# Steps of a chunked scan traced at their places in a stream of dense matmuls, one turn four triples later, and a scaling moved behind a convolution

## The chip, the cores and the metric

The kernel runs on one core of a Trainium2 chip. The metric is the device time of one execution in microseconds (us). The kernel before was timed three times. The profile is of one further execution, and times within it count from the start of its span.

## The reference

One hybrid encoder over 512 tokens of width 1024: a Mamba-2 layer, then a differential attention layer, all in fp32. The change lies in the first layer, cut here to what matters:

```python
def mamba2_layer(x, norm_g, w_in, conv_w, conv_b, dt_bias, a_log, d_skip, gate_norm_g, w_out):
    h = rms_norm(x, norm_g)
    zxbcdt = h @ w_in                                   # z | x | B | C | dt
    ...
    xbc = jax.nn.silu(causal_depthwise_conv(xbc, conv_w, conv_b))
    xs, bm, cm = ...                                    # 8 groups: 4 heads of 64, state 128
    dt = jax.nn.softplus(dt_raw + dt_bias)
    a = -jnp.exp(a_log)
    y = ssd_chunked_scan(xs * dt[..., None], a * dt, bm, cm)
    y = y + d_skip * xs
    y = gated_group_rms_norm(y, z, gate_norm_g)         # y * silu(z), norm within a group
    return x + y @ w_out
```

The scan, per chunk: `y = (C B^T * decay) x + (C state) * exp(acs)` and `state = state * exp(acs_end) + B^T (x * to_end)`, where `acs` is the running sum of `a * dt`. The second layer (shared K/V, queries, two softmax maps per head, ALiBi, a gate and an output projection) and the final norm follow.

## The kernel before

**Dense stream.** A product in fp32 precision is made of three matmuls on operands split into a high and a low part (`mm3`: high times high, high times low, low times high). I call three such matmuls a triple. The first layer's projections are one stream of triples, in the order `z0 g0 g1 z1 g2 g3 z2 g4 o0 g5 z3 g6 g7 o1 o2 o3`: `z` is a quarter of z, token-major (32 triples), `g` one group's B, C and two halves of x, feature-major (32 triples), `o` a quarter of the output projection. Each item fills four PSUM banks of a pool of four (`mm`), named pz, pg and po in the trace. A bank is free again when its last reader is done: for pz ScalarE's silu (zs), for po VectorE's add to x_tok, for pg VectorE's convolution.

**Weights.** Each item has two loads of 1 MB (raw). ScalarE writes the high part, scaled by the norm's gain (whi, four pieces), and VectorE the low part (wlo). Raw, whi and wlo have two buffers each, so whi of an item waits until TensorE has used the weights two loads earlier.

**Convolution.** `conv` takes a bank pg: VectorE scales it by the norm's row, ScalarE starts xc with one tap and the bias, VectorE adds three taps (scalar_tensor_tensor, 511, 510 and 509 columns wide), ScalarE applies silu. The step with 509 columns is the last to read the bank. B's tile is the first of a group, then C's, then the two of x.

**Scan.** `ssd(g)` handles one group in steps, with TensorE's part of each: `cb` (C B^T, into pcb), `bt` (three transposes of B, pbt), `xt` (eight transposes of x, pxt; VectorE then scales x into xdt and dx), `st` (state products psA and psB on xe, which GpSimd makes from xdt; then 64 small products pyd), `o1` and `o2` (state times C, po1 and po2; VectorE scales them into tmp), and `yt`, the turn (pyt): eight transposes of the normed result tmp, read by ScalarE into yh and by VectorE into yl. Between o2 and yt lies the gated norm: GpSimd adds tmp to dx, VectorE multiplies by zs, ScalarE squares, VectorE takes a root in ten small steps (v, y_i, y_y, y_c), ScalarE writes the scaled tmp. `decays` loads the running sums of a group (dec), and GpSimd subtracts and masks them (four affine selects), ScalarE takes exp. Scan banks come from a pool of three (`ss`) and one bank of their own (`long`).

**Order.** A table, PLACES, gives each step of each group a number of triples after the end of that group's projection. In the kernel before, a group's whole scan is written when its projection has been written; the wrapper `Ordered` logs TensorE's instructions with their step, and `in_places` sorts the log by the table and chains TensorE's instructions in that order. On the other engines a scheduler orders instructions by the dependencies and the order in which the code wrote them.

Of the kernel before, what the change touches and what calls it, by code (L numbers as in the profile page):

```python
# [22 lines left out]
G = 8  # L23
# [24 lines left out]
    "y0": (None,) * 7 + (69,),  # L48
# [15 lines left out]
class Ordered:  # L64


    def __init__(self, tc, engine):
        self.tc, self.engine, self.on = tc, engine, False
        self.step, self.log = None, None

    def __getattr__(self, name):
        op = getattr(self.engine, name)

        def call(*args, **kw):
            i = op(*args, **kw)  # L75
            if self.on:
                self.tc.keep_in_program_order(i)
            elif self.log is not None:
                self.log.append((self.step, i.ins))
            return i  # L80
# [5 lines left out]
def trunk(ctx, tc, x, x_t, par, w_dt, w_in, w_out, w_kvqg, w_bo, d_skip, lam_qk, fin_g, out):  # L86
# [405 lines left out]
    ps_tt = ss_bank("ps_tt")  # L492
    for i, src in enumerate((dtp, acs, toe)):
        T.transpose(ps_tt[:, i * P:(i + 1) * P], src, ident)
    tok = const.tile([P, 4, NQ, H], F32, name="tok")
    V.tensor_copy(tok[:, 0:3].rearrange("p a c h -> p (a c h)"), ps_tt[:, 0:3 * P])
    A.activation(tok[:, 3], tok[:, 1], AF.Exp)
    dt_tok, acs_tok, toe_tok, eacs_tok = (tok[:, i] for i in range(4))


# [18 lines left out]

    def conv(ps, ft, name, bufs):  # L520
# [7 lines left out]
        for k in (2, 1, 0):  # L528
            d = 3 - k
            V.scalar_tensor_tensor(out=xc[:, d:], in0=u[:, :S - d], scalar=cw[k], in1=xc[:, d:], op0=ALU.mult, op1=ALU.add)  # L530
# [44 lines left out]
    def stream_a():  # L575
        for it in order_a[1:]:
            j = int(it[1])
            yield from {"z": z_proj, "g": group_proj, "o": out_proj}[it[0]](j)
            done.add(it)
            ends[it] = sum(step is None for step, i in T.log)  # L580
        while True:
            yield

    ends = {}

    def in_places(log):

        dense = [i for step, i in log if step is None]
        parts = {}
        for step, i in log:  # L590
            if step:
                parts.setdefault(step, []).append(i)
        due = sorted((ends[f"g{g}"] + 3 * PLACES[kind][g], n, kind, g) for n, (kind, g) in enumerate(parts))
        order = []
        for n, i in enumerate(dense + [None]):
            while due and due[0][0] <= n:
                order += parts[due.pop(0)[2:]]
            order.append(i)
# [27 lines left out]
    def ssd(g):  # L626
# [5 lines left out]
        T.step = "cb", g  # L632
# [4 lines left out]
        T.step = "bt", g  # L637
# [26 lines left out]
        T.step = "st", g  # L664
# [58 lines left out]
        for j, a in [(j, a) for a in range(0, NQ, n) for j in range(2)]:  # L723
            T.step = f"y{a}" if g == G - 1 else "yt", g
# [512 lines left out]
```

## Time and profile before

| | |
|---|---|
| median of three runs | 713.04 us (712.07 to 714.62) |
| profiled execution | 712.19 us, span 710.4 us |
| TensorE busy | 697.7 us (98%) |
| VectorE busy | 520.5 us (73%) |
| ScalarE busy | 426.9 us (60%) |
| GpSimd busy | 113.9 us (16%) |
| dense matmul, 128x512 | 390 to 403 ns each, pipelined |
| TensorE clock granted | full in all 40 slices |

In a row of the timeline the first number is the start, the second the time from the start of the first to the end of the last instruction of that row, then engine, line, operation, output and inputs, and count. Brackets give the engine's idle time ahead and what ended it. All operations of TensorE, VectorE and ScalarE stand on line 75, the wrapper's call, so tiles identify them. Matmul ends are modelled and overlap, so the distance between starts shows the pace.

### The profile page before, as it was taken

To read this page: it belongs to the slowest core of one execution; us is meant where nothing else is said; L and a number is where in the kernel's file an instruction comes from. 1 tells how busy PE (TensorE), PEld (TensorE's weight loads), DVE (VectorE), ACT (ScalarE), POOL (GpSimd) and SP (SyncE) were. 2 spreads that over 40 slices of the span, in tenths; PEclk is the share of its full clock that TensorE was granted. 3 is DMA by queue.
4 is the path that set the end of the run, shared out by engine and by line. 5 is a ranking of instruction groups with operands and counts; after the bars stand their busy time and mean duration, and the time that the engine had idled before them with its cause. 6 is when DMAs were issued, how large, how long until landed. Compare 5 with 4: busy or idle time off the path is not lost.

```text
span 710.4 us, 10484 instructions
## 1 busy us (share of the span) xinstructions
PE 697.7 (98%) x3838; PEld 579.8 (82%) x3838; DVE 520.5 (73%) x1181; ACT 426.9 (60%) x931; POOL 113.9 (16%) x158
## 2 busy tenths in 40 slices
PE   8999999999999999999999999999999999999996
PEld 7878878887788888888788878888888888888884
DVE  5579964888579669558996856457768657788786
ACT  6839662664653636537635347557777667765556
POOL 0108421502405025041110101000000000000002
PEclk9999999999999999999999999999999999999999
DMA  8643313333043241231122310322211221113003
GB/s 293 254 172 130 119 59 120 118 118 120 16 163 119 83 150 66 97 140 60 60 69 110 119 60 17 149 81 88 91 60 66 82 90 60 62 57 119 31 1 118
DMA packets 13491, 70.85 MB, mean 100 GB/s; under 512 B 1792, under 2 KB 3328, under 8 KB 6016
## 3 DMA queue, kind: packets, MB, share of 16 engines
q1 hardware_dynamic: 13008, 69.90, 26.8%
q8 instruction: 30, 0.49, 0.3%
q10 hardware_dynamic: 432, 0.28, 0.1%
q14 instruction: 21, 0.17, 0.1%
HBM read 68.02 MB, written 2.16 MB: 99 GB/s over the span
## 4 chain that ended last, share of the span: by engine, by line
PE 91%; DVE 4%; ACT 2%; issue 1%; POOL 1%; DMA 1%; ACTq 0%; POOLq 0%
PE pg L75 23%; PE po L75 16%; PE pz L75 10%; PE pt L75 7%; PE pq L75 6%; PE pk L75 6%; PE pv L75 6%; PE pb L75 3%; PE sc L75 3%; PE pyd L75 2%; PE pc L75 2%; PE psA L75 1%; DVE xc L75 1%; PE pcb L75 1%; DVE wlo L75 1%
## 5 line engine op out<-in xcount | busy, mean ns | idle before, releaser
L75 DVE SCALAR_TENSOR_TENSOR wlo<-raw,prm,whi 128x512 fp32r<-128x512 f32 (+1 forms) x240 | 149.5, 672 | 53.5 <-ACT whi L75 52.7
L75 ACT ACTIVATE whi<-raw,prm 128x512 fp32r<-128x512 f32 (+1 forms) x240 | 133.6, 628 | 52.2 <-PE pg L75 11.7
L75 PE MATMUL pg<-a_hi,whi 128*128 128x512 f32 x256 | 103.2, 403 | 0.1
L75 PE MATMUL pg<-a_hi,wlo 128*128 128x512 f32 x256 | 100.2, 391 | 0.1
L75 PE MATMUL pg<-a_lo,whi 128*128 128x512 f32 x256 | 99.9, 390 | 0.0
L75 DVE SCALAR_TENSOR_TENSOR xc<-pg,prc,xc 128x511 f32<-128x511 f32 (+2 forms) x96 | 69.8, 740 | 6.6 <-ACT xc L75 6.1
L75 PEld LDWEIGHTS pg<-a_hi,wlo 128*128 128x128 f32 x256 | 48.1, 188 | 11.0 <-DVE wlo L75 0.5
L75 PEld LDWEIGHTS pg<-a_hi,whi 128*128 128x128 f32 x256 | 48.1, 188 | 10.2 <-issue 0.7
L75 PEld LDWEIGHTS pg<-a_lo,whi 128*128 128x128 f32 x256 | 48.2, 188 | 9.4
L75 PE MATMUL po<-whi,yh 128*128 128x512 f32 x128 | 51.6, 403 | 1.3 <-DVE xc L75 1.3
L75 PE MATMUL pz<-whi,a_hi 128*128 128x512 f32 x128 | 49.8, 398 | 1.7 <-DVE xc L75 1.3
L75 PE MATMUL po<-whi,yl 128*128 128x512 f32 x128 | 50.1, 391 | 0.0
L75 PE MATMUL po<-wlo,yh 128*128 128x512 f32 x128 | 50.0, 390 | 0.0
L75 PE MATMUL pz<-whi,a_lo 128*128 128x512 f32 x128 | 48.9, 390 | 0.0
L75 PE MATMUL pz<-wlo,a_hi 128*128 128x512 f32 x128 | 48.9, 390 | 0.0
L1042 POOL TENSOR_TENSOR ot<-x_tok,fg 128x512 f32<-128x512 f32 x4 | 5.0, 1292 | 248.9 <-DVE x_tok L75 248.9
L75 ACT ACTIVATE s<-s,mx 128x128 f32<-128x128 f32 (+3 forms) x64 | 35.6, 557 | 10.1 <-DVE mx L75 10.0
L657 POOL TENSOR_TENSOR xe<-xdt,tok 128x256 f32<-128x256 f32 x24 | 14.1, 615 | 165.0 <-DVE xdt L75 165.0
L75 DVE CUSTOM_DVE_ANT_0 s<-sc,bias 128x128 f32<-128x128 f32 (+3 forms) x64 | 29.3, 487 | 15.3 <-PE sc L75 14.8
L75 ACT ACTIVATE xc<-pg,prc 128x512 f32<-128x512 f32 x32 | 24.8, 776 | 25.3 <-DVE pg L75 19.9
L75 ACT ACTIVATE xc<-xc 128x512 f32<-128x512 f32 x32 | 20.0, 629 | 27.0 <-DVE xc L75 22.5
L75 ACT ACT_TABLE_LOAD x23 | 29.5, 1283 | 10.6 <-DVE xc L75 9.1
(238 smaller groups left out, 1629.9 us busy)
## 6 DMA issues: line engine op xcount, KB each, us to landing
raw<-in_w_in SPq DMA_DIRECT2D x22, 1024.0 KB, 4.8
raw<-in_w_kvqg SPq DMA_DIRECT2D x16, 1024.0 KB, 4.8
dec<-acs_d SPq DMA_DIRECT2D x8, 1024.0 KB, 4.9
raw<-in_w_out SPq DMA_DIRECT2D x8, 1024.0 KB, 4.8
raw<-in_w_bo SPq DMA_DIRECT2D x4, 1024.0 KB, 4.8
x_tok<-in_x SPq DMA_DIRECT2D x4, 512.0 KB, 8.9
out<-ot SPq DMA_DIRECT2D x6, 256.0 KB, 2.1
raw<-in_w_in SPq DMA_DIRECT2D x4, 256.0 KB, 4.7
```

The source lines that it names most:

```text
L75: i = op(*args, **kw)
L657: GP.tensor_tensor(out=xe[:, c], in0=xdt[:, c], in1=toe_tok[:, c, hs].unsqueeze(2).to_broadcast([P, R, HD]), op=ALU.mult)
L1042: GP.tensor_tensor(out=o, in0=y, in1=f, op=ALU.mult)
```

## The change

The steps of the scan become yields of `ssd`: a step is written when the stream of triples has come to its place (`first_layer`, `resume`), and TensorE simply keeps program order, so that the log and the sorting are gone. The transposition of dt and the sums (`turned`, ps_tt), with the first two `decays`, becomes such a step at triple 22. The table moves group 0's bt from 3 to 10, group 0's turn from 56 to 60 and group 1's bt from 24 to 28 (the same place in the stream as that turn). Group 7's first turn keeps 69, in a row shared with the others. Where steps fall on one triple, the older group's came first; now the order follows from when the steps were entered in the queue and how long it was then. In the built order the younger group's step comes first at groups 2 and 3 (pcb3 before po12 and po22, pbt3 before pyt2) and at groups 6 and 7 (pcb7 before po16, pbt7 before pyt6). And x's scaling (xdt, dx) may be issued only after the last convolution step of the next group's B tile, where that is already written.

```diff
@@ -39,13 +39,12 @@
 PLACES = {
     "cb": (10, 2, 14, 14, 5, 5, 14, 12),
-    "bt": (3, 24, 21, 44, 35, 25, 21, 37),
+    "bt": (10, 28, 21, 44, 35, 25, 21, 37),
     "xt": (16, 35, 31, 52, 43, 36, 31, 43),
     "st": (25, 47, 37, 63, 53, 47, 36, 53),
     "o1": (28, 47, 46, 64, 54, 47, 44, 53),
     "o2": (32, 52, 46, 69, 60, 52, 47, 58),
-    "yt": (56, 85, 76, 99, 89, 85, 69, None),
-    "y0": (None,) * 7 + (69,),
+    "y0": (60, 85, 76, 99, 89, 85, 69, 69),
     "y2": (None,) * 7 + (72,),
 }
@@ -489,14 +485,17 @@
         z_out(0, t, pz0[t])
-    ps_tt = ss_bank("ps_tt")
-    for i, src in enumerate((dtp, acs, toe)):
-        T.transpose(ps_tt[:, i * P:(i + 1) * P], src, ident)
     tok = const.tile([P, 4, NQ, H], F32, name="tok")
-    V.tensor_copy(tok[:, 0:3].rearrange("p a c h -> p (a c h)"), ps_tt[:, 0:3 * P])
-    A.activation(tok[:, 3], tok[:, 1], AF.Exp)
     dt_tok, acs_tok, toe_tok, eacs_tok = (tok[:, i] for i in range(4))
+    def turned():
+        yield "tt"
+        ps_tt = ss_bank("ps_tt")
+        for i, src in enumerate((dtp, acs, toe)):
+            T.transpose(ps_tt[:, i * P:(i + 1) * P], src, ident)
+        V.tensor_copy(tok[:, 0:3].rearrange("p a c h -> p (a c h)"), ps_tt[:, 0:3 * P])
+        A.activation(tok[:, 3], tok[:, 1], AF.Exp)
+        decays((0, 1))
     def runs_of(kind):
@@ conv @@
+    conv_end = {}
...
@@ -527,7 +528,7 @@
         A.activation(xc, u, AF.Identity, scale=cw[3], bias=prc[:, ft:ft + 1])
         for k in (2, 1, 0):
             d = 3 - k
-            V.scalar_tensor_tensor(out=xc[:, d:], in0=u[:, :S - d], scalar=cw[k], in1=xc[:, d:], op0=ALU.mult, op1=ALU.add)
+            conv_end[ft] = V.scalar_tensor_tensor(out=xc[:, d:], in0=u[:, :S - d], scalar=cw[k], in1=xc[:, d:], op0=ALU.mult, op1=ALU.add)
         A.activation(xc, xc, AF.Silu)
         return xc
@@ -572,34 +573,30 @@
                     sq = small.tile([P, S], F32, tag="wide", name=f"sq3_{t}", bufs=2)
                     A.activation(sq, x_tok[:, t, ns], AF.Square, accum_out=bss[:, 0, t:t + 1])
-    def stream_a():
+    due = []
+
+    def resume(n, at, gen, places):
+        kind = next(gen, None)
+        if kind is not None:
+            due.append((at + places[kind], len(due), at, gen, places))
+
+    def first_layer():
+        n = 0
         for it in order_a[1:]:
             j = int(it[1])
-            yield from {"z": z_proj, "g": group_proj, "o": out_proj}[it[0]](j)
-            done.add(it)
-            ends[it] = sum(step is None for step, i in T.log)
-        while True:
-            yield
-
-    ends = {}
-
-    def in_places(log):
-
-        dense = [i for step, i in log if step is None]
-        parts = {}
-        for step, i in log:
-            if step:
-                parts.setdefault(step, []).append(i)
-        due = sorted((ends[f"g{g}"] + 3 * PLACES[kind][g], n, kind, g) for n, (kind, g) in enumerate(parts))
-        order = []
-        for n, i in enumerate(dense + [None]):
-            while due and due[0][0] <= n:
-                order += parts[due.pop(0)[2:]]
-            order.append(i)
-        order.pop()
+            for _ in {"z": z_proj, "g": group_proj, "o": out_proj}[it[0]](j):
+                n += 1
+                due.sort(key=lambda e: e[:2])
+                while due and due[0][0] <= n:
+                    place, _, at, gen, places = due.pop(0)
+                    with tc.high_priority() if places.get("last") else ExitStack():
+                        resume(n, at, gen, places)
+                    due.sort(key=lambda e: e[:2])
+            if it[0] == "g":
+                places = {kind: p[j] for kind, p in PLACES.items()}
+                places["last"] = j == G - 1
+                resume(n, n, ssd(j), places)
         assert not due
-        for i, before in zip(order[1:], order):
-            tc.add_manual_dep(i, before.name, mybir.DependencyInfo(mybir.DependencyClass.NoSync, mybir.DependencyReason.DATA), reason="order")
     bss = small.tile([P, 2, NT], F32, name="bss", bufs=1)
     decs = {}
@@ -642,16 +639,18 @@
         A.copy(bt.rearrange("p c n -> p (c n)"), pbt[:, 0:3 * P])
         xdt = bp.tile([P, NQ, R, HD], F32, tag="xdt", name=f"xdt{g}")
         dx = bp.tile([P, NQ, R, HD], F32, tag="dx", name=f"dx{g}")
-        T.step = "xt", g
+        yield "xt"
         for j in range(2):
             pxt = ss_bank(f"pxt{g}_{j}")
             for c in range(NQ):
                 T.transpose(pxt[:, c * P:(c + 1) * P], xc[j][:, c * P:(c + 1) * P], ident)
             pv = pxt.rearrange("p (c h e) -> p c h e", h=2, e=HD)
             h2 = slice(R * g + 2 * j, R * g + 2 * j + 2)
-            V.tensor_tensor(out=xdt[:, :, 2 * j:2 * j + 2, :], in0=pv, in1=dt_tok[:, :, h2].unsqueeze(3).to_broadcast([P, NQ, 2, HD]), op=ALU.mult)
-            V.tensor_tensor(out=dx[:, :, 2 * j:2 * j + 2, :], in0=pv,
-                            in1=dsk[:, h2].unsqueeze(1).unsqueeze(3).to_broadcast([P, NQ, 2, HD]), op=ALU.mult)
+            next_b = conv_end.get(17 + g)
+            with tc.issue_after(next_b.ins) if next_b else ExitStack():
+                V.tensor_tensor(out=xdt[:, :, 2 * j:2 * j + 2, :], in0=pv, in1=dt_tok[:, :, h2].unsqueeze(3).to_broadcast([P, NQ, 2, HD]), op=ALU.mult)
+                V.tensor_tensor(out=dx[:, :, 2 * j:2 * j + 2, :], in0=pv,
+                                in1=dsk[:, h2].unsqueeze(1).unsqueeze(3).to_broadcast([P, NQ, 2, HD]), op=ALU.mult)
         xe = bp.tile([P, 3, R, HD], F32, tag="xe", name=f"xe{g}")
         for c in range(3):
             GP.tensor_tensor(out=xe[:, c], in0=xdt[:, c], in1=toe_tok[:, c, hs].unsqueeze(2).to_broadcast([P, R, HD]), op=ALU.mult)
@@ -721,29 +720,19 @@
         n = 2 if g == G - 1 else NQ
         for j, a in [(j, a) for a in range(0, NQ, n) for j in range(2)]:
-            T.step = f"y{a}" if g == G - 1 else "yt", g
+            if not j:
+                yield f"y{a}"
             for c in range(a, a + n):
                 T.transpose(pyt[j][:, c * P:(c + 1) * P], tm[:, c, j * P:(j + 1) * P], ident)
             cs = slice(a * P, (a + n) * P)
             A.copy(yh[:, j, cs], pyt[j][:, cs])
             V.tensor_tensor(out=yl[:, j, cs], in0=pyt[j][:, cs], in1=yh[:, j, cs].bitcast(F32), op=ALU.subtract)
         yT[g] = (yh, yl)
-        T.step = None
-
-    decays((0, 1))
-    dense[0] = stream_a()
-    T.log = []
-    for g in range(G):
-        until(f"g{g}")
-        if g < G - 1:
-            ssd(g)
-        else:
-            with tc.high_priority():
-                ssd(g)
-    until("o3")
-    in_places(T.log)
-    T.log = None
-
+
+    T.on = True
+    resume(0, 0, turned(), {"tt": 22})
+    first_layer()
+    T.on = False
     hh, hl = new_h("b")
     done.clear()
```

**ScalarE around group 0's turn**, in z1. zs is the silu of z, whi8 and whi9 are weights of g2. Before:

```order
L75 ACTIVATE tmp0_697<-dx0_662,y_y_754 128x256 x4
L75 CAST yh0_770<-pyt0_0_772 128x512
L75 CAST yh0_770<-pyt0_1_773 128x512
L75 COPY bt1_947<-pbt1_943 128x384
L75 ACTIVATE whi8_924<-raw8_922,prm_70 128x512 x4
L75 ACTIVATE zs1_2_0_1218<-pz1_2_1173,ar_col_239 128x256
```

and with the change:

```order
L73 ACTIVATE tmp0_798<-dx0_702,y_y_883 128x256 x4
L73 ACTIVATE whi8_912<-raw8_910,prm_70 128x512 x4
L73 ACTIVATE zs1_2_0_1055<-pz1_2_990,ar_col_239 128x256
L73 ACTIVATE zs1_2_1_1057<-pz1_2_990,ar_col_239 128x256
L73 CAST yh0_899<-pyt0_0_901 128x512
L73 CAST yh0_899<-pyt0_1_902 128x512
```

The turn's readers yh and the copy of bt now stand behind the four pieces of whi8 and the two halves of zs1_2. On TensorE the turn itself moved from behind the third triple of pz1_3 to behind the last triple of pz1_2, twelve matmuls later.

**VectorE at the end of g3**, ahead of z2. xc19 is B's tile on bank pg3_0, xc27 C's on pg3_1, xc6 one of x's. Before:

```order
L75 SCALAR_TENSOR_TENSOR xc19_1620<-pg3_0_1402,prc_72,xc19_1620 128x510
L75 SCALAR_TENSOR_TENSOR xc27_1633<-pg3_1_1551,prc_72,xc27_1633 128x510
L75 TENSOR_TENSOR xdt2_1417<-pxt2_0_1419,tok_438 128x4x128
L75 TENSOR_TENSOR dx2_1418<-pxt2_0_1419,dsk_344 128x4x128
L75 SCALAR_TENSOR_TENSOR xc19_1620<-pg3_0_1402,prc_72,xc19_1620 128x509
L75 TENSOR_TENSOR xdt2_1417<-pxt2_1_1426,tok_438 128x4x128
L75 TENSOR_TENSOR dx2_1418<-pxt2_1_1426,dsk_344 128x4x128
L75 SCALAR_TENSOR_TENSOR xc6_1652<-pg3_2_1588,prc_72,xc6_1652 128x511
L75 SCALAR_TENSOR_TENSOR xc27_1633<-pg3_1_1551,prc_72,xc27_1633 128x509
```

and with the change:

```order
L73 SCALAR_TENSOR_TENSOR xc19_1497<-pg3_0_1390,prc_72,xc19_1497 128x510
L73 SCALAR_TENSOR_TENSOR xc27_1510<-pg3_1_1403,prc_72,xc27_1510 128x510
L73 SCALAR_TENSOR_TENSOR xc19_1497<-pg3_0_1390,prc_72,xc19_1497 128x509
L73 TENSOR_TENSOR xdt2_1492<-pxt2_0_1545,tok_434 128x4x128
L73 TENSOR_TENSOR dx2_1493<-pxt2_0_1545,dsk_344 128x4x128
L73 TENSOR_TENSOR xdt2_1492<-pxt2_1_1552,tok_434 128x4x128
L73 TENSOR_TENSOR dx2_1493<-pxt2_1_1552,dsk_344 128x4x128
L73 SCALAR_TENSOR_TENSOR xc6_1529<-pg3_2_1440,prc_72,xc6_1529 128x511
L73 SCALAR_TENSOR_TENSOR xc27_1510<-pg3_1_1403,prc_72,xc27_1510 128x509
```

The last step on bank pg3_0 (xc19, 128x509) moved ahead of both xdt and dx; the last step on pg3_1 stays where it was. VectorE's order at the end of g7, ahead of o1, changes in the same way.

**VectorE in z2, before g4.** v42, y_i, y_y and y_c are the root of group 2's norm, and wlo14 and wlo15 are weights of g4. Before:

```order
L75 TENSOR_TENSOR y_c_1511<-y_y_1510,v42_1508 128x4
L75 TENSOR_TENSOR y_c_1511<-y_c_1511,y_y_1510 128x4
L75 SCALAR_TENSOR_TENSOR y_c_1511<-y_c_1511 128x4
L75 SCALAR_TENSOR_TENSOR y_y_1510<-y_c_1511,y_y_1510 128x4
L75 TENSOR_TENSOR y_c_1511<-y_y_1510,v42_1508 128x4
L75 TENSOR_TENSOR y_c_1511<-y_c_1511,y_y_1510 128x4
L75 SCALAR_TENSOR_TENSOR y_y_1510<-y_c_1511,y_y_1510 128x4
L75 SCALAR_TENSOR_TENSOR wlo14_1681<-raw14_1678,prm_70,whi14_1680 128x512 x4
L75 SCALAR_TENSOR_TENSOR wlo15_1895<-raw15_1892,prm_70,whi15_1894 128x512 x4
```

and with the change:

```order
L73 TENSOR_TENSOR y_c_1724<-y_y_1723,v42_1721 128x4
L73 SCALAR_TENSOR_TENSOR wlo14_1582<-raw14_1579,prm_70,whi14_1581 128x512
L73 TENSOR_TENSOR y_c_1724<-y_c_1724,y_y_1723 128x4
L73 SCALAR_TENSOR_TENSOR wlo14_1582<-raw14_1579,prm_70,whi14_1581 128x512
L73 SCALAR_TENSOR_TENSOR y_c_1724<-y_c_1724 128x4
L73 SCALAR_TENSOR_TENSOR wlo14_1582<-raw14_1579,prm_70,whi14_1581 128x512
L73 SCALAR_TENSOR_TENSOR y_y_1723<-y_c_1724,y_y_1723 128x4
L73 SCALAR_TENSOR_TENSOR wlo14_1582<-raw14_1579,prm_70,whi14_1581 128x512
L73 TENSOR_TENSOR y_c_1724<-y_y_1723,v42_1721 128x4
L73 TENSOR_TENSOR y_c_1724<-y_c_1724,y_y_1723 128x4
L73 SCALAR_TENSOR_TENSOR y_y_1723<-y_c_1724,y_y_1723 128x4
L73 SCALAR_TENSOR_TENSOR wlo15_1667<-raw15_1664,prm_70,whi15_1666 128x512 x4
```

The four pieces of wlo14 now stand between the steps of the root, where they stood behind its last step. A little ahead of these rows, dec3 times pcb3 now comes before tmp2, as pcb3 now comes before po12 and po22 on TensorE. ScalarE's squares of the last two quarters (ss42) moved from ahead of the exponential of dec4 to behind it, and GpSimd does three of dec4's four masks ahead of its first addition for group 2.

More of the change, by code (lines that the diff above doesn't have):

```diff
@@ L68, in __init__ @@
         self.tc, self.engine, self.on = tc, engine, False
-        self.step, self.log = None, None
     def __getattr__(self, name):
@@ L77, in call @@
                 self.tc.keep_in_program_order(i)
-            elif self.log is not None:
-                self.log.append((self.step, i.ins))
             return i
@@ L630, in ssd @@
         hs = slice(R * g, R * g + R)
-        T.step = "cb", g
+        yield "cb"
         pcb = long_bank(f"pcb{g}")
@@ L636, in ssd @@
             T.matmul(pcb[:, cs], lhsT=bc[:, cs], rhs=cc[:, cs], start=True, stop=True)
-        T.step = "bt", g
+        yield "bt"
         pbt = ss_bank(f"pbt{g}")
@@ L663, in ssd @@
         psA = ss_bank(f"psA{g}")
-        T.step = "st", g
+        yield "st"
         for c in range(2):
@@ L690, in ssd @@
             decays((g + 1, g + 2))
-        T.step = "o1", g
+        yield "o1"
         po1 = ss_bank(f"po1{g}")
         T.matmul(po1[:, 256:512], lhsT=cc[:, P:2 * P], rhs=hsf[:, 0], start=True, stop=True)
-        T.step = "o2", g
+        yield "o2"
         po2 = ss_bank(f"po2{g}")
@@ L774, in last_rows @@
             row_norm(t, po)
-    due = [0.0]
+    owed = [0.0]
     def beside(n):
-        due[0] += n
-        while due[0] > 0:
-            due[0] -= next(dense[0], due[0])
+        owed[0] += n
+        while owed[0] > 0:
+            owed[0] -= next(dense[0], owed[0])
     T.on = V.on = A.on = True
@@ L971, in trunk @@
     dense[0] = paced(stream_b())
-    due[0] = 0.0
+    owed[0] = 0.0
     beside(8)
@@ L1076, in trunk @@
     until("q0t0")
-    due[0] = 0.0
+    owed[0] = 0.0
     last = None
```

## The prediction

> **What bounds the kernel now.** I read the page's busy times first, then TensorE's own waits, then the timeline around each wait.
>
> ```profile
> span 710.4 us, 10484 instructions
> PE 697.7 (98%) x3838; PEld 579.8 (82%) x3838; DVE 520.5 (73%) x1181; ACT 426.9 (60%) x931; POOL 113.9 (16%) x158
> PE pyt L75 <- ACT tmp L75: 1.5, 1, 1.5
> PE pz L75 <- DVE xc L75: 1.3, 1, 1.3
> PE po L75 <- DVE xc L75: 1.3, 1, 1.3
> ```
>
> TensorE sets the time: it is without work for only 710.4 - 697.7 = 12.7 us. Work taken from another engine is worth nothing unless it ends a wait of TensorE. The three waits shown are the only ones inside the first layer; the others lie at the kernel's start and in its tail, which the diff does not touch. So the change is worth what it does to these three, less any wait it makes.
>
> **Part 1: group 0's last turn, four triples later.** Here is TensorE at the turn (pyt), with an undisturbed turn of group 2 below it.
>
> ```profile
> 99.38 0.39 PE L75 MATMUL pz<-whi,a_lo 128*128 128x512 f32 x1
> 101.27 1.97 PE L75 MATMUL pyt<-ident,tmp 128*128 128x128 f32 x8 [1.51 <-ACT tmp L75]
> 103.32 0.47 PE L75 MATMUL pz<-whi,a_hi 128*128 128x512 f32 x1
> 199.01 1.04 PE L75 MATMUL pyt<-ident,tmp 128*128 128x128 f32 x8
> 200.13 0.48 PE L75 MATMUL pg<-a_hi,whi 128*128 128x512 f32 x1
> ```
>
> The idle figure says 1.51, but the starts say more. Dense matmuls start 0.23 apart (twelve of them from 162.75 to 165.54, rows in part 2), and a free turn with its three transposes of bt takes 200.13 - 199.01 = 1.12. From 99.38 to 103.32 there are 3.94, so this turn lost 3.94 - 0.23 - 1.12 = **2.59 us**: the transposes that follow also wait, one by one, for ScalarE's four writes of tmp, and count as busy meanwhile. The Trainium skill (Perfetto Trace Analysis, Identifying the Most-Contended Engine) warns that matmul busy time misleads because matmuls are pipelined; the trace agrees here, 1.51 idle against 2.59 lost. By the idle figure alone the sum below would be 2.86 instead of 3.94.
>
> Does tmp come early enough for the new place? The turn would start at 99.38 + 0.23 + 12 x 0.23 = 102.37. ScalarE and VectorE around it:
>
> ```profile
> 100.71 1.71 ACT L75 ACTIVATE tmp<-dx,y_y 128x256 f32<-128x256 f32 x4 [0.77 <-DVE y_y L75]
> 102.84 1.08 ACT L75 CAST yh<-pyt 128x512 fp32r<-128x512 f32 x2 [0.42 <-PE pyt L75]
> 104.29 2.56 ACT L75 ACTIVATE whi<-raw,prm 128x512 fp32r<-128x512 f32 x4
> 106.76 0.81 ACT L75 ACTIVATE zs<-pz,ar_col 128x256 f32<-128x256 f32 x2
> 103.46 1.29 DVE L75 TENSOR_TENSOR yl<-pyt,yh 128x512 fp32r<-128x512 f32 x2 [2.78 <-ACT yh L75]
> 110.92 1.04 PE L75 MATMUL pxt<-ident,xc 128*128 128x128 f32 x8
> ```
>
> The first transpose started 0.13 after the first quarter of tmp could be done (100.71 + 0.43 = 101.14). The fourth quarter ends at 102.42, so it is usable at 102.55; the fourth transpose comes at 102.37 + 3 x 0.10 = 102.67. No wait is left, with 0.12 to spare. What is late next is the reading of the turn: ScalarE now does the next weights' four whi and two zs first (102.42 + 2.47 + 0.81 = 105.70), then yh, and VectorE's first yl starts 0.62 after yh (102.84 to 103.46) and takes 0.65: 106.97. Queued behind are TensorE's transposes of x for group 1 (pxt), the next to need that bank, at 110.92 - 2.59 = 108.33. Cover 1.36 us; beyond it each us is a us of TensorE. I take the full 2.59; the lower bound is the plain idle of 1.51. The weights themselves gain, since whi now starts at 102.42 instead of 104.29. Group 0's bt and the three start-up transposes (ps_tt) only move among dense matmuls of 0.23 and nobody waited for them: 0, between -0.1 and +0.15, a switch or so saved.
>
> **Part 2: x's scaling behind the next group's first bank.** The scaling moves at two places only, ahead of z2 and ahead of o1. First place, VectorE and TensorE:
>
> ```profile
> 160.67 0.68 DVE L75 TENSOR_TENSOR xdt<-pxt,tok 128x512 f32<-128x512 f32 x1
> 161.87 0.73 DVE L75 SCALAR_TENSOR_TENSOR xc<-pg,prc,xc 128x509 f32<-128x509 f32 x1
> 162.52 0.68 DVE L75 TENSOR_TENSOR xdt<-pxt,tok 128x512 f32<-128x512 f32 x1
> 163.72 1.39 DVE L75 SCALAR_TENSOR_TENSOR xc<-pg,prc,xc 128x511 f32<-128x511 f32 x2
> 162.75 0.47 PE L75 MATMUL pz<-whi,a_hi 128*128 128x512 f32 x1 [1.30 <-DVE xc L75]
> 165.54 0.39 PE L75 MATMUL pz<-whi,a_hi 128*128 128x512 f32 x1
> ```
>
> TensorE starts 162.75 - 161.87 = 0.88 after the last convolution step of B's bank starts. That step moves into the place of the first xdt, 160.67, so z2 starts at 161.55: 1.20 earlier. But z2 wants its second bank 165.54 - 162.75 = 2.79 later, at 164.34, and that bank is freed by the second of the two steps at 163.72, which starts at 164.38 and does not move, since the work ahead of it is the same: 164.38 + 0.88 = 165.26. A new wait of 0.92 takes the place of most of the old one, and z2 keeps **0.28**. The second xdt still starts at 162.52, so GpSimd's xe, which waits for it, is not late.
>
> Second place:
>
> ```profile
> 346.74 0.68 DVE L75 TENSOR_TENSOR xdt<-pxt,tok 128x512 f32<-128x512 f32 x1
> 347.93 0.73 DVE L75 SCALAR_TENSOR_TENSOR xc<-pg,prc,xc 128x509 f32<-128x509 f32 x1
> 349.78 1.39 DVE L75 SCALAR_TENSOR_TENSOR xc<-pg,prc,xc 128x511 f32<-128x511 f32 x2
> 348.81 0.47 PE L75 MATMUL po<-whi,yh 128*128 128x512 f32 x1 [1.30 <-DVE xc L75]
> 351.66 1.03 PE L75 MATMUL psA<-xe,bt 128*128 128x256 f32 x4
> 355.07 0.50 PE L75 MATMUL po<-whi,yh 128*128 128x512 f32 x1
> 349.35 1.76 POOL L657 TENSOR_TENSOR xe<-xdt,tok 128x256 f32<-128x256 f32 x3 [26.60 <-DVE xdt L75]
> ```
>
> Again 0.88 behind the step (347.93 to 348.81), now from 346.74: o1 starts at 347.62, **1.19** earlier. Here the second bank is wanted only after the scan's psA, psB and pyd, at 355.07 - 1.19 = 353.88, and is free at 349.78 + 0.66 + 0.88 = 351.32. The third is released by the add of o1's first bank to x_tok, which stood at 355.00 and now stands one row earlier; o1 wants it four triples of 0.68 after 353.88, at 356.60. Next to be late is xe: its second part ends at 349.35 + 2 x 0.59 = 350.53, and psA's second product now falls at 351.66 - 1.19 + 0.22 = 350.69. That is 0.16 of cover. I take 1.19; bounds 0.28, if a bank is waited for as at z2, and 1.30, the idle shown.
>
> **Part 3: exchanged ties.** Where two steps fall on one triple, the younger group's now goes first: pcb before po, pbt before pyt (groups 2/3 and 6/7). At groups 2/3 this reorders VectorE, GpSimd and ScalarE ahead of g4's weights:
>
> ```profile
> 181.35 0.64 POOL L619 TENSOR_SCALAR_AFFINE_SELECT dec<-dec 128x512 f32<-128x512 f32 x1
> 181.96 0.74 POOL L707 TENSOR_TENSOR dx<-dx,tmp 128x256 f32<-128x256 f32 x1
> 184.80 1.61 POOL L619 TENSOR_SCALAR_AFFINE_SELECT dec<-dec 128x512 f32<-128x512 f32 x2
> 182.73 0.83 DVE L75 TENSOR_TENSOR dx<-dx,zs 128x256 f32<-128x256 f32 x1 [1.95 <-POOL dx L707]
> 186.47 1.28 ACT L75 ACT_TABLE_LOAD   x1
> 189.59 2.54 ACT L75 ACTIVATE whi<-raw,prm 128x512 fp32r<-128x512 f32 x4
> 190.33 2.74 DVE L75 SCALAR_TENSOR_TENSOR wlo<-raw,prm,whi 128x512 fp32r<-128x512 f32 x4 [1.89 <-ACT whi L75]
> 191.14 0.50 PE L75 MATMUL pg<-a_hi,wlo 128*128 128x512 f32 x1
> ```
>
> GpSimd now does three masks (0.61 each, 181.35 to 181.96), one dx (0.68) and the last mask (0.64): 184.50 instead of 184.80 + 1.61 = 186.41. ScalarE's square of the product that follows dx (183.86 + 0.05, then 0.83, then 0.42) ends at 185.2; table load and exp take 189.59 - 186.47 = 3.12, two squares that stood ahead of them now follow, 0.42 each: whi starts at 189.2, 0.4 sooner. VectorE's wlo now stands between the small steps of the root: four of 0.2 ahead, first wlo at 190.0 (was 190.33), then one per 0.66 + 0.12, the fourth at 192.36 (was 190.33 + 3 x 0.66 = 192.31). TensorE's use follows wlo by 0.81 (190.33 to 191.14): fourth at 193.17, where before its pace gave 191.14 + 3 x 0.73 = 193.33. So of the 0.28 won at z2 **0.16** stays. The norm of tmp now ends behind whi (2.45), a load (1.30), zs, whi and zs (4.1) and itself (1.71) at 198.8; the turn, moved behind pbt, needs its fourth quarter at 199.4. At groups 6/7 the same exchange reorders VectorE's adds and scan steps from 354 on, but the norm ended there at 375.3 and its turn came at 379.9: over 4 us of cover, so 0. If this cover fails, each us that the last mask slips beyond 0.4 is a us of TensorE.
>
> **Sum.** 2.59 + 0.16 + 1.19 = 3.94 us. The profiled execution took 712.19 (span 710.4 and 1.8 around it), so 708.25 for such a one. The median of the runs shown, 713.04, lies 0.85 above it; the forecast is **709.1**. Runs of this kernel spread over 712.07 to 714.62, and 0.3%, 2.1 us, is what a measurement can tell from no change.
>
> **Rivals.**
>
> *The lead is handed back.* VectorE is nearly full where the second wait stands:
>
> ```profile
> 150.00:166.00 16.00, 14.70 (x76) 12.08 (x74) 15.19 (x25) 10.96 (x20) 1.76 (x3) 1.00 0.17 67
> 124.60 2.56 ACT L75 ACTIVATE whi<-raw,prm 128x512 fp32r<-128x512 f32 x4 [3.16 <-PE pg L75]
> ```
>
> VectorE is busy 15.19 of 16.00 us. If it cannot move, TensorE's 2.59 return as a longer wait at z2, and 0.16 + 1.19 = 1.35 are left: 711.7, no change. Against it: at 124.60 ScalarE had waited 3.16 us for TensorE to release the weight buffer, and VectorE's train of work starts from those weights, so it moves along. Chance 0.10.
>
> *A second term fails.* o1 keeps only 0.28 like z2, or g4's weights come a us late: gain about 2.9, 710.1. For it: the covers of 0.16 and 0.12 are small. Chance 0.14.
>
> *The moves don't free what they say.* The two banks wait for something besides the step shown: 2.59 alone, 710.4. Against it: TensorE starts 0.88 after that step at both places. Chance 0.05.
>
> *Slower through GpSimd.* If GpSimd's five operations before g4 run as long as its worst neighbour in such company,
>
> ```profile
> 353.18 1.72 POOL L668 TENSOR_TENSOR hst<-hst,dec 128x256 f32<-128x256 f32 x1 [2.07 <-ACT hst L75]
> ```
>
> five times 1.72 = 8.6 replaces 184.50 - 181.35 = 3.15. The last mask is 5.45 late, whi 5.05 later than before, and TensorE stands as long: 713.04 - 2.59 - 1.19 + 5.05 = 714.3. It decides once the last mask is later than 184.50 + 0.4 + 3.78 = 188.7, where the gain is gone. Against it: the same masks took 0.64 to 0.81 beside VectorE's work before. The Trainium skill (SBUF — State Buffer, SBUF: two separate sides) says GpSimd and a VectorE operation with two SBUF inputs lock each other out. The row above, beside wlo, fits that; the masks would meet only one such operation, which would make it 0.83 late at most, and by that rule the sum loses about 0.4. Chance 0.04.
>
> **How the numbers follow.** Forecast 0.67, with its own range 708.3 to 710.0 (the parts' small bounds and half the spread of the runs). The 0.8 range reaches from 707.6 to the handed-back case: 707.6 to 711.8. Faster by over 0.3%: 0.65 of the forecast, 0.12 and 0.04 of the two cases between, together 0.81. Within: 0.10 and the remainders, 0.16. Slower: 0.03.
>
> **What would show it.** In the changed profile the wait of pyt for tmp is gone, and pyt stands about 2.7 us after the matmul where it stood. z2 shows a wait of about 0.1 at its first bank and 0.7 to 0.9 at its second. o1 starts without a wait of 1.3. pg of g4 is no later against z2's end. Wrong would be: pxt of group 1 waiting for yl, psA waiting for xe, a longer wait at z2's first bank (handed back), or whi of g4 after 190 on the old clock.

## The result, and the profile after

The changed kernel took 708.90 us in the median of six runs (708.22 to 709.19), the kernel before 712.93 (711.99 to 714.62, six runs): 4.03 us less, a ratio of 0.9941 with the 95% interval 0.9928 to 0.9955. The forecast was 709.1. The profiled execution took 709.16 with a span of 707.4, where 708.25 was forecast for it.

From the page and from TensorE's waits, after:

```profile
span 707.4 us, 10489 instructions
PE 697.1 (99%) x3838; PEld 579.8 (82%) x3838; DVE 519.5 (73%) x1181; ACT 426.2 (60%) x931; POOL 113.4 (16%) x158
PE pz L73 <- DVE xc L73: 0.7, 1, 0.7
PE pg L73 <- DVE xc L73: 0.4, 1, 0.4
PE pg L73 <- ACT zs L73: 0.4, 1, 0.4
```

The wait of pyt for tmp is gone, and so is that of po. The wait of pz (z2) for a bank has shrunk from 1.3 to 0.7 and now stands at the second bank. Two waits of 0.4 are new; they lie at 31.0 and 53.9 us, ahead of the turn, which is the first of the three places that the prediction counts.

The timeline of TensorE, ScalarE and VectorE at the turn, after:

```profile
102.73 0.39 PE L73 MATMUL pz<-whi,a_lo 128*128 128x512 f32 x1
102.96 1.04 PE L73 MATMUL pyt<-ident,tmp 128*128 128x128 f32 x8
104.08 0.48 PE L73 MATMUL pz<-whi,a_hi 128*128 128x512 f32 x1
100.57 1.71 ACT L73 ACTIVATE tmp<-dx,y_y 128x256 f32<-128x256 f32 x4 [0.77 <-DVE y_y L73]
105.35 1.05 ACT L73 CAST yh<-pyt 128x512 fp32r<-128x512 f32 x2
105.96 1.29 DVE L73 TENSOR_TENSOR yl<-pyt,yh 128x512 fp32r<-128x512 f32 x2 [0.29 <-ACT yh L73]
108.96 1.03 PE L73 MATMUL pxt<-ident,xc 128*128 128x128 f32 x8
```

The turn now takes 104.08 - 102.96 = 1.12, as a free one does, and its first yl is done at 106.61, 2.35 ahead of the pxt that needs its bank.

At z2 and at o1, after:

```profile
159.30 0.68 DVE L73 TENSOR_TENSOR xdt<-pxt,tok 128x512 f32<-128x512 f32 x1
161.69 1.40 DVE L73 SCALAR_TENSOR_TENSOR xc<-pg,prc,xc 128x511 f32<-128x511 f32 x2
159.53 0.47 PE L73 MATMUL pz<-whi,a_hi 128*128 128x512 f32 x1
162.13 0.39 PE L73 MATMUL pz<-whi,a_lo 128*128 128x512 f32 x1
163.24 0.47 PE L73 MATMUL pz<-whi,a_hi 128*128 128x512 f32 x1 [0.72 <-DVE xc L73]
345.73 0.47 PE L73 MATMUL po<-whi,yh 128*128 128x512 f32 x1
348.56 1.03 PE L73 MATMUL psA<-xe,bt 128*128 128x256 f32 x4
347.46 1.75 POOL L656 TENSOR_TENSOR xe<-xdt,tok 128x256 f32<-128x256 f32 x3 [26.63 <-DVE xdt L73]
```

Both first banks come without a wait. z2's second bank is late by 163.24 - 162.13 - 0.23 = 0.88 by the starts.

To see where time came from I compare the start of the same dense matmul in two profiles. The marks are starts before: M0 = 99.38 (last before the turn's old place), M1 = 106.38 (behind its new place), M2 = 161.05 (last of g3), M3 = 175.68 (z2, behind both banks), M4 = 193.09 (g4, fourth triple), M5 = 347.11 (last of g7), M6 = 348.81 (first of o1). The table gives, for the kernel after and for the experiments below, by how many us a profile differs from before at each mark (minus: earlier). The experiments were timed in three groups, each beside the kernel before; the last column has that kernel's median, with which a median is best compared.

| kernel | M0 | M1 | M2 | M3 | M4 | M5 | M6 | median us | before beside it |
|---|---|---|---|---|---|---|---|---|---|
| after | +0.63 | -1.98 | -2.02 | -2.23 | -1.95 | -1.89 | -3.08 | 708.90 | 712.93 |
| e1 turn back | -0.38 | -0.55 | -0.59 | -0.81 | -0.57 | -0.53 | -1.72 | 710.79 | 712.99 |
| e2 no scaling moved | +0.46 | -2.15 | -2.09 | -2.04 | -2.12 | -2.02 | -2.01 | 710.01 | 712.99 |
| e3 old ties | -0.50 | -3.11 | -3.10 | -3.31 | -3.14 | -3.13 | -4.32 | 708.16 | 712.99 |
| e4 tracing alone | +0.48 | +0.50 | +0.67 | +0.72 | +0.91 | +0.94 | +0.94 | 713.28 | 712.99 |
| e5 after again | -0.02 | -2.63 | -2.53 | -2.74 | -2.47 | -2.40 | -3.59 | 709.01 | 712.64 |
| e6 scaling at o1 only | +1.25 | -1.36 | -1.41 | -1.40 | -1.63 | -1.56 | -2.76 | 708.62 | 712.64 |
| e7 dx behind C | -0.20 | -2.81 | -2.85 | -4.00 | -4.46 | -4.03 | -5.21 | 707.84 | 712.64 |
| e8 dx behind C, old ties | +0.54 | -2.07 | -2.09 | -3.26 | -3.72 | -3.74 | -4.92 | 706.68 | 712.64 |
| e9 whi14 first | +0.04 | -2.57 | -2.56 | -2.78 | -3.25 | -2.53 | -3.72 | 708.52 | 712.02 |
| e10 turn at 64 | +0.08 | - | -0.75 | -0.96 | -0.84 | -0.77 | -1.96 | 709.96 | 712.02 |
| e11 turn at 58 | -0.14 | -1.82 | -1.58 | -1.80 | -1.57 | -1.45 | -2.64 | 709.26 | 712.02 |

For after: the turn gains 2.61 (M0 to M1), z2 gains 0.21 (M2 to M3), g4 takes 0.34 back (M3 to M5), o1 gains 1.19 (M5 to M6). With 0.04 between M1 and M2 that is 3.71 of the 3.94 forecast. This execution began 0.63 late (M0), which is why its span shrank by 3.0 only.

### The profile page after: what moved, and what is told of

Same layout as the page of the kernel before. It is cut to its first block, busy times and chain, and to the rows that moved or that the text cites. A ratio compares the mean times of both kernels' runs of the same rounds, so it can differ in the third digit from the quotient of the medians.

```text
span 707.4 us, 10489 instructions
## 1 busy us (share of the span) xinstructions
PE 697.1 (99%) x3838; PEld 579.8 (82%) x3838; DVE 519.5 (73%) x1181; ACT 426.2 (60%) x931; POOL 113.4 (16%) x158
## 3 DMA queue, kind: packets, MB, share of 16 engines
HBM read 68.02 MB, written 2.16 MB: 99 GB/s over the span
## 4 chain that ended last, share of the span: by engine, by line
PE 88%; DVE 4%; DMA 3%; ACT 2%; issue 1%; POOL 1%; SPq 0%; ACTq 0%; POOLq 0%
PE pg L73 23%; PE po L73 16%; PE pt L73 8%; PE pz L73 7%; PE pq L73 6%; PE pk L73 6%; PE pv L73 6%; PE pb L73 3%; DMA raw<-in_w_in 3%; PE sc L73 3%; PE pyd L73 2%; PE pc L73 2%; DVE wlo L73 1%; PE pcb L73 1%; PE psA L73 1%
```

## The experiments

**e1 and e2: one part of the change undone.** Against the changed kernel, e1's edit:

```diff
-    "bt": (10, 28, 21, 44, 35, 25, 21, 37),
+    "bt": (10, 24, 21, 44, 35, 25, 21, 37),
-    "y0": (60, 85, 76, 99, 89, 85, 69, 69),
+    "y0": (56, 85, 76, 99, 89, 85, 69, 69),
```

and e2's:

```diff
-            next_b = conv_end.get(17 + g)
+            next_b = None
```

> The changed kernel with the turn of group 0 back at 56 and the transposes of B of group 1 back at 24; the rest of the change stays. If the turn is worth its 2.59 us and adds to the rest: 708.9 + 2.6 = 711.5, the turn waits about 1.5 us for tmp again, and o1 still starts without a wait for the convolution. If a lead of TensorE in z1 is handed back by the next weights or by z2's banks: 709.9 or less. If the turn carries the whole gain: 712.9.

> The changed kernel with x's scaling unbound again at both places. If z2 keeps only about 0.2 of its bank's 1.2 us and o1 keeps all 1.19: 708.9 + 1.4 = 710.3, with 1.3 us of waiting at the first bank of z2 and of o1 again and none at z2's second bank. If both places are worth their whole idle: 708.9 + 2.5 = 711.4. If the moved scaling frees nothing that counts: 708.9.

e1 took 710.79 us (709.72 to 713.14), 1.9 more than the changed kernel, and e2 710.01 (709.51 to 712.15), 1.1 more. TensorE's waits in e1:

```profile
PE pyt L73 <- ACT tmp L73: 1.3, 1, 1.3
PE pz L73 <- DVE xc L73: 0.7, 1, 0.7
```

and in e2:

```profile
PE pz L73 <- DVE xc L73: 1.3, 1, 1.3
PE po L73 <- DVE xc L73: 1.3, 1, 1.3
```

Each part brings its own wait back and leaves the other's alone. In the table e1 has nothing of the turn's gain (-0.17, tmp stood 0.18 earlier there against M0), all of o1's; e2 has 2.61 at the turn and nothing at o1. The parts add up. Both times are below what was expected, by 0.7 and 0.3; the traces do not show a smaller price for either part (M0 to M6, e1 gains 1.34 and e2 2.47, against 3.71).

**e3 and e4: the older group first, and tracing alone.** e4 has e1's and e2's edits, e3's, and bt of group 0 at 3.

```diff
-            due.append((at + places[kind], len(due), at, gen, places))
+            due.append((at + places[kind], at, at, gen, places))
```

> The changed kernel with the older group's step first again where two steps fall on one triple. The trace after showed that the products po of group 2 now come 0.89 later behind pcb3, and that 0.34 us are given up at g4's first weights. Theory: the exchange costs this 0.34, since GpSimd's work on dec4 waits for po and the four wlo14 stand between root steps; without it 708.9 - 0.3 = 708.6, and from the start of z2's second bank to the first matmul of g4's fourth triple it is 27.3 (before) instead of 27.7. Rival, as the prediction had it: the exchange brings the weights 0.4 sooner and costs 0.1: 708.8 to 709.1, the same distance as after or more.

> The changed kernel with all four other things undone: the turn at 56, bt at 3 and 24, no binding of the scaling, the older group first. What is left is that steps are traced at their places, with ps_tt in one piece and pbt0 behind pcb0. If tracing itself moves nothing that counts: 712.9 within 0.5. If a part of the gain comes from the new way of writing: 712 or less.

e4 took 713.28 us (711.88 to 715.65), ratio to before 1.0001 (0.9989 to 1.0013): writing the steps at their places is worth nothing that the times can tell, and the gain belongs to the turn, the scaling and the order of ties. By the trace e4 ends 0.46 behind from M0 to M6, 0.27 of it between M2 and M5. In e4 the transposes of B of group 0 stand right behind pcb0, as in the changed kernel, so e4 holds that move and the move of ps_tt too.

e3 took 708.16 (707.82 to 708.54), 0.7 less than the changed kernel; its ratio to before, 0.9926 (0.9913 to 0.9939), is not clear of the changed kernel's. And its trace does not bear out the theory. It loses at g4 as well (M3 to M5 +0.18), and the distance named in the expectation is 27.56, not 27.3. In the table it won most of its lead ahead of M0, where nothing is different. The reason for g4's loss is in the chain of dec4: its load, GpSimd's first instruction on it, and the weights whi14. Before, after and in e3, from the timelines of SP's queue, GpSimd and ScalarE, and for after the fourth wlo14 on VectorE (whi and wlo of before are shown in the prediction):

```profile
170.73 0.33 SPq L614 DMA_DIRECT2D dec<-acs_d  x1
177.04 0.20 POOL L616 COPY dec<-dec 128x8 f32<-128x8 f32 x1 [6.35 <-PE po L75]
```

```profile
168.71 0.33 SPq L611 DMA_DIRECT2D dec<-acs_d  x1
175.31 0.19 POOL L613 COPY dec<-dec 128x8 f32<-128x8 f32 x1 [6.63 <-PE po L73]
187.46 2.55 ACT L73 ACTIVATE whi<-raw,prm 128x512 fp32r<-128x512 f32 x4
190.50 0.75 DVE L73 SCALAR_TENSOR_TENSOR wlo<-raw,prm,whi 128x512 fp32r<-128x512 f32 x1
```

```profile
167.62 0.33 SPq L611 DMA_DIRECT2D dec<-acs_d  x1
173.92 0.19 POOL L613 COPY dec<-dec 128x8 f32<-128x8 f32 x1 [6.32 <-DMA dec<-acs_d]
186.45 2.55 ACT L73 ACTIVATE whi<-raw,prm 128x512 fp32r<-128x512 f32 x4
```

From copy to whi it is 12.55 before, 12.15 after and 12.53 in e3: the exchange of ties does bring the weights 0.40 sooner, as the prediction had it, and my theory that it delays them through po falls. The other half of that theory, the small steps of the root between the wlo14, costs about what the prediction took for it: the fourth wlo14 starts 1.81 sooner than before (190.33 + 3 x 0.66 = 192.31 to 190.50) where whi14 starts 2.13 sooner, and M4 has 1.95. Where the profile names po as the releaser, I take the load for the cause, since the copy starts 0.1 behind its landing. The view of transfers gives its time from issue to landing, before and after:

```profile
dec<-acs_d SPq DMA_DIRECT2D x1, 1024.0 KB, 6.2
```

```profile
dec<-acs_d SPq DMA_DIRECT2D x1, 1024.0 KB, 6.5
```

168.71 + 6.5 = 175.2, and the copy starts at 175.31. The load is issued 2.02 sooner than before, which is TensorE's lead at M2, and the same holds in e1 (0.59 sooner) and e3 (3.11). What z2 wins behind M2 does not reach it, because SP's queue waits there for GpSimd's last product for the state:

```profile
SPq L611 <- POOL hst L671: 1.1, 1, 1.1
```

So the new theory: g4's weights stand behind dec4, dec4's load stands behind the state of group 2, and z2's 0.21 is handed back at g4. The 0.3 by which this load took longer comes on top, and uses up most of the 0.40 that the ties win.

**e5 and e6: the changed kernel again, and the scaling moved only ahead of o1.**

```diff
-            next_b = conv_end.get(17 + g)
+            next_b = conv_end.get(17 + g) if g == 6 else None
```

> The changed kernel itself once more, beside the next three on the same chip. 708.9 within 0.5. Its first matmuls came 0.55 to 0.86 us late in the first profile, behind a weight load that landed 0.87 us later than before. If that lateness belongs to one execution, the profile now shows another value between -0.3 and +0.6; if it belongs to the program, about the same 0.6 ahead of the turn.

> The changed kernel with x's scaling bound only for group 6 (ahead of o1), unbound ahead of z2. Theory: what z2 keeps, 0.2 us, is handed back at g4, because the load of dec4 follows VectorE's sums for the scan state, which do not come sooner; so this kernel equals the changed one within 0.1 (708.9), z2 shows 1.3 us at its first bank and none at its second, and from the end of g3 to the second triple row of g4 it takes as long as after. Rival: z2's part stays to the end, then it is 0.2 to 0.3 slower, 709.2; rival with the bank's full 1.2: 710.1.

e5: 709.01 us (708.24 to 710.05), and M0 at -0.02. The late start of the first profile belonged to that execution. All stages behind M0 agree with the first profile to 0.15 us.

e6: 708.62 (708.05 to 711.14). z2 keeps nothing there (M2 to M3 +0.01), and yet M2 to M5 is -0.15, against +0.13 in after and in e5. The moved scaling ahead of z2 is worth nothing to the end. By these traces it would cost 0.28, but the load of dec4 took 6.2 in e6 and 6.5 in after and e5, and that accounts for the difference. The profiles in which whi14 stands behind dec4, with the time from the issue of this load to GpSimd's copy:

| kernel | first at ties | issue to copy | M2 to M5 |
|---|---|---|---|
| before | older | 6.31 | 0 |
| e3 | older | 6.30 | -0.03 |
| e4 | older | 6.55 | +0.27 |
| e6 | younger | 6.32 | -0.15 |
| e10 | younger | 6.44 | -0.02 |
| e2 | younger | 6.51 | +0.07 |
| e1 | younger | 6.55 | +0.06 |
| e11 | younger | 6.56 | +0.13 |
| after, e5 | younger | 6.60 | +0.13 |

What is lost up to M5 grows with the load's time, and at an equal load the younger group first is 0.1 to 0.2 better. Ahead of z2 the scaling is unbound in before, e2, e4 and e6 and bound in the others, and that makes no difference that can be seen here. Why the load took longer in some profiles is not shown.

**e9: the weights of g4 ahead of dec4.** To test the theory by itself, dec4's table load and exponential are put behind whi14 on ScalarE. One thing moved with it: the scheduler also put the norm of tmp (group 2's) ahead of whi15 and of the second pair of zs, where it stands behind them in the changed kernel.

```diff
-                    A.activation(hi[:, k, :], raw[:, k, :], AF.Copy, scale=gains[k])
+                    whi_end[i] = A.activation(hi[:, k, :], raw[:, k, :], AF.Copy, scale=gains[k])
...
         for g in gs:
-            A.activation(decs[g][2], decs[g][2], AF.Exp)
+            with tc.issue_after(whi_end[14].ins) if g == 4 else ExitStack():
+                A.activation(decs[g][2], decs[g][2], AF.Exp)
```

> The changed kernel with one order exchanged on ScalarE alone: the four whi14 (g4's first weights) ahead of dec4's table load and exponential. Theory: what z2 keeps is lost at g4 because whi14 waits there behind dec4, whose load does not come sooner; now whi14 starts about 2 us earlier, g4's first four triples run without waiting, and from the start of z2's second bank to the second matmul of g4's fourth triple it is 27.2 us instead of 27.9: 708.2. Rival: VectorE's wlo14 between the root's steps sets g4's start, and the distance stays within 0.2 of 27.9: 708.9.

The timeline of e9 at g4:

```profile
184.79 2.55 ACT L73 ACTIVATE whi<-raw,prm 128x512 fp32r<-128x512 f32 x4
189.85 0.39 PE L73 MATMUL pg<-a_lo,whi 128*128 128x512 f32 x1
...
192.61 1.70 ACT L73 ACTIVATE tmp<-dx,y_y 128x256 f32<-128x256 f32 x4
196.67 0.82 ACT L73 ACTIVATE zs<-pz,ar_col 128x256 f32<-128x256 f32 x2
197.54 0.50 PE L73 MATMUL pg<-a_hi,whi 128*128 128x512 f32 x1 [0.43 <-ACT zs L73]
```

and the same zs and norm after:

```profile
194.51 0.83 ACT L73 ACTIVATE zs<-pz,ar_col 128x256 f32<-128x256 f32 x2
195.22 1.70 ACT L73 ACTIVATE tmp<-dx,y_y 128x256 f32<-128x256 f32 x4
```

whi14 starts 184.79, and g4's first matmuls follow each other without a wait. From z2's second bank (162.69) to the fourth triple's second matmul it is 27.16, as expected, against 27.90 in after and 27.55 before. That g4's start waits for whi14 behind dec4 is shown. But the price was wrong: a bank of z2 is freed at 197.5 by ScalarE's zs, and of the 0.47 won at M4 and the 0.22 of z2 nothing is left at M5 (M2 to M5, -2.56 to -2.53). The time is 708.52 (707.82 to 709.57), 0.3 above the expectation and not distinguishable from the changed kernel's. dec4's exponential stands ahead of this zs in the changed kernel as well. New ahead of it is the norm of tmp: it makes up 1.60 (192.61 to 194.21) of the 2.16 by which zs starts later than in after. So what dec4's order alone is worth up to M5, e9 does not show.

**e7 and e8: z2's second bank freed as well.** dx waits for the next group's C tile, so that both xdt and the last step on the second bank come ahead of it; e8 adds e3's line.

```diff
...
+            next_c = conv_end.get(25 + g)
+            with tc.issue_after(next_c.ins) if next_c else ExitStack():
                 V.tensor_tensor(out=dx[:, :, 2 * j:2 * j + 2, :], in0=pv,
...
```

> The changed kernel with one step more: dx (the second product of x's scaling) is bound behind the next group's C tile, so that xdt and the last step on the second bank come ahead of both dx. The scheduler then also puts whi14 ahead of dec4's table load and exponential on ScalarE. Theory: z2's wait at its second bank (0.9) goes, and g4's weights no longer follow dec4, so that g4's first twelve matmuls gain about 0.7: 707.3. If VectorE hands the 0.9 back elsewhere (as a wait of psA for xe, or for the next bank): 708.2. If both fail: 708.9.

> As the kernel with dx behind the C tile, and with the older group's step first again, by which whi14 stays behind dec4's exponential. Theory that dec4's load sets the start of g4: the 0.9 won at z2's second bank comes back as waiting at g4's first weights, and the time is that of the changed kernel with old ties, 708.2 to 708.9, about 1 us above the kernel with dx behind C alone. If g4's weights move with TensorE: 707.5 to 707.9 and no longer waits at g4 than before.

e7: 707.84 us (706.99 to 708.46); e8: 706.68 (706.36 to 708.38), ratio to before 0.9913 (0.9892 to 0.9934), and 2.3 below the changed kernel beside it (e5). At z2 in e8, VectorE and TensorE:

```profile
159.24 1.28 DVE L73 TENSOR_TENSOR xdt<-pxt,tok 128x512 f32<-128x512 f32 x2
160.43 1.39 DVE L73 SCALAR_TENSOR_TENSOR xc<-pg,prc,xc 128x511 f32<-128x511 f32 x2
162.29 0.39 PE L73 MATMUL pz<-whi,a_hi 128*128 128x512 f32 x1
182.55 2.57 ACT L73 ACTIVATE whi<-raw,prm 128x512 fp32r<-128x512 f32 x4 [0.45 <-PE pz L73]
186.43 1.92 ACT L73 ACTIVATE dec<-dec 128x2056 f32<-128x2056 f32 x1
```

The second bank's last step starts at 161.09 instead of 162.35, and the wait is gone: z2 wins 1.15 in e7 and 1.17 in e8. In both, the scheduler put whi14 ahead of dec4's exponential. I had that wrong for e8, whose expectation rests on the contrary, so e8 does not test the theory of dec4. Together they show that z2 keeps its lead where g4's weights don't follow dec4. e7 loses 0.43 of it again behind M4, at group 2's turn:

```profile
194.85 1.47 PE L73 MATMUL pyt<-ident,tmp 128*128 128x128 f32 x8
```

A free turn takes 1.04 there; the norm of tmp (193.80 to 195.51 on ScalarE) came too late. In e8 that norm stands ahead of whi15 and the turn is free, so that M2 to M5 gives 1.65. Why e8 is 1.2 faster than e7 by the medians while the traces differ by 0.47 there stays open.

**e10 and e11: the turn's place.** e10's edit; e11 has 26 and 58 in the same two places.

```diff
-    "bt": (10, 28, 21, 44, 35, 25, 21, 37),
+    "bt": (10, 32, 21, 44, 35, 25, 21, 37),
-    "y0": (60, 85, 76, 99, 89, 85, 69, 69),
+    "y0": (64, 85, 76, 99, 89, 85, 69, 69),
```

> The changed kernel with group 0's turn four triples later still (64, and the transposes of B of group 1 at 32). ScalarE then reads the turn behind the next four whi9 as well. Theory (what is late next are the readers): yh starts near 109.7 instead of 105.4, yl ends near 111, and the transposes of x for group 1, which need that bank at 109.0, wait about 2 us: 711.0. Rival: the bank has cover enough, or those transposes use another: 708.9.

> The changed kernel with group 0's turn two triples earlier (58, and the transposes of B of group 1 at 26). Theory: tmp's last quarter is usable at 102.55 on the clock of before, and the fourth transpose would come at 101.27, so 1.2 us of the 2.59 are lost again where the start of the run is as in before: 710.1; 0.5 where TensorE starts 0.6 late as in the first profile after. Rival: the turn's loss was not a wait for tmp that ends at a fixed time, and 58 is as good as 60: 708.9.

e10: 709.96 us (709.43 to 711.36). Its timeline:

```profile
105.13 1.04 PE L73 MATMUL pyt<-ident,tmp 128*128 128x128 f32 x8
108.51 1.06 ACT L73 CAST yh<-pyt 128x512 fp32r<-128x512 f32 x2
109.11 1.29 DVE L73 TENSOR_TENSOR yl<-pyt,yh 128x512 fp32r<-128x512 f32 x2 [0.29 <-ACT yh L73]
109.86 1.09 PE L73 MATMUL pxt<-ident,xc 128*128 128x128 f32 x8 [1.30 <-DVE yl L73]
```

The readers are late next, as the prediction said: pxt waits for yl, 1.30 us by the idle figure. By the starts it is 1.51: against before, the dense matmul ahead of pxt is 2.51 sooner and the one behind it 1.00. About 2 were expected; whi9, which in both kernels follows a wait for pz, began 1.8 earlier than in after (105.33 against 107.11), with the turn's 1.12 now behind that point.

e11: 709.26 (708.41 to 710.00). Here tmp is late again:

```profile
100.24 1.71 ACT L73 ACTIVATE tmp<-dx,y_y 128x256 f32<-128x256 f32 x4 [0.78 <-DVE y_y L73]
100.82 1.95 PE L73 MATMUL pyt<-ident,tmp 128*128 128x128 f32 x8
```

The turn takes 1.95 instead of 1.04, and M0 to M1 gives 1.68 instead of 2.61: 0.93 lost. The expectation said 1.2; tmp stood 0.33 earlier against M0 than before (100.24 + 0.14 against 100.71), which is the difference. Both theories hold, and 60 lies between the two cliffs. The medians of e10 and e11 are 1.1 and 0.4 above the changed kernel's, but the kernel before was 0.9 faster beside them than beside it. Against before, e10 gains 2.06 and e11 2.76, where the changed kernel gained 4.03 and, in e5, 3.63. The traces say the same: 2.04 and 2.50 from M0 to M6, against 3.71 and 3.57.

## Why the prediction was right

- **The time.** 709.1 forecast, 708.90 measured, by the mechanism named: the sum was 3.94, the medians differ by 4.03, and the trace shows 3.71 from M0 to M6. That the time came out to 0.2 is in part luck, since the start alone scatters by more than that between profiles (M0), and the single profiled execution missed its own forecast by 0.9.
- **Part 1, the turn: 2.59 by the starts, not 1.51 by the idle figure.** Measured 2.61 in all eight profiles with the turn at 60, whatever else was changed. The slack was larger than the 0.12 of the prediction: in e5 tmp's last quarter can be used 0.8 ahead of its transpose, as tmp starts 0.8 earlier against TensorE; why it does is not shown. The readers had 2.35 of cover, not 1.36. e11 and e10 show what lies at either side.
- **Part 2, z2: keeps 0.28 of 1.20, with a new wait of 0.92 at the second bank.** Measured 0.21 and 0.88, and no wait at the first bank, where the prediction expected one of about 0.1; e7 and e8, which free the second bank, win 1.15 and 1.17.
- **Part 2, o1: 1.19.** Measured 1.19 in after, e1, e3, e5 and e9, and 0 in e2. The cover of xe was 0.16; in after its second part ends at 347.46 + 2 x 0.585 = 348.63 and psA's second product starts at 348.56 + 0.22 = 348.78. It held, by 0.15.
- **Part 3, "of the 0.28 won at z2 0.16 stays"** is the step that failed, by a size and not by its mechanism. From M2 to M5 after and e5 end 0.13 behind instead of 0.16 ahead, and g4 comes later against z2's end (0.28 from M3 to M4), where the prediction named "no later" as a sign. The prediction already counted g4's weights on the clock ahead of z2, and so it is: in after dec4's load is issued 2.02 sooner, the lead at M2. From there it had 0.4 for the masks in a row, and 0.40 came; it had the small steps between the wlo14 take 0.24 of that, and from whi14 to M4 0.18 went, with another 0.06 up to M5. What it put at nothing without a reason is the time of dec4's load: GpSimd's copy starts only 1.73 sooner, so 0.29 is lost there. In e6, with the same order and the load as fast as before, 0.15 stays. It is a small case of the rival that a lead is handed back, at g4 and not at z2.
- **The moves among dense matmuls, 0.** e4's time confirms it to 0.3 us; its trace cannot show it, since these moves lie ahead of M0.
- **Slower through GpSimd** did not happen: the three masks in a row took 1.81, 0.60 each.

Not explained: the gains of e1 and e3 against before, 2.20 and 4.83 by the medians, where their traces show 1.34 and 3.82 from M0 to M6.

## What to carry to other kernels

Price a wait of TensorE by the distance between starts and a free neighbour, not by the idle figure: here 2.59 against 1.51, and 2.61 came out. Before counting a won bank, ask when the next one is wanted and what sets the start of the next weights: z2's first bank was worth 1.2 us by itself, 0.2 with the second bank behind it, and nothing at g4, whose weights waited for a load that stands behind the work ahead of z2. Compare two profiles mark by mark at the same matmul, since the start of an execution can hide or feign half a microsecond and more, and compare a median with the kernel before that was timed beside it.

## What the runs showed of the hardware

The same matmul at M0 stood between -0.50 and +1.25 us of its time before in twelve profiles whose programs differ little up to there; in after, ScalarE's first whi behind the load of raw began at 26.27 instead of 25.40, with 2.98 instead of 2.42 of waiting for that load:

```profile
26.27 2.56 ACT L73 ACTIVATE whi<-raw,prm 128x512 fp32r<-128x512 f32 x4 [2.98 <-DMA raw<-in_w_in]
```

One load of 1 MB took 4.9 to 6.5 us from issue to landing in these runs (dec4's: 4.9 in e7, 6.2 before, 6.5 after).

GpSimd's first product for the state took 1.29 us in after, the first 0.80 of it beside VectorE's wlo; the second, with no wlo beside it, took 0.62:

```profile
165.53 1.29 POOL L667 TENSOR_TENSOR hst<-hst,dec 128x256 f32<-128x256 f32 x1 [2.50 <-ACT hst L73]
168.06 0.62 POOL L671 TENSOR_TENSOR hst<-hst,dec 128x256 f32<-128x256 f32 x1 [1.25 <-DVE hst L73]
163.60 2.73 DVE L73 SCALAR_TENSOR_TENSOR wlo<-raw,prm,whi 128x512 fp32r<-128x512 f32 x4
```

The Trainium skill (SBUF — State Buffer, SBUF: two separate sides) says that GpSimd and a VectorE operation with two SBUF inputs lock each other out. These rows fit it without proving it: the product starts at 165.53, wlo ends at 166.33, and 166.33 + 0.62 = 166.95 is near the 166.82 at which the product ends.
